# A pad of 32 bytes in place of 96 at the top of SBUF, and another order of scalings and stores in the last tile

## The chip, the cores and the metric

One core of one Trainium2 chip. The metric is device time in microseconds (us) of one execution of the program, the median of several runs.

## What is computed

One encoder layer for 512 positions of width 2048, all in float32:

```python
h = rms_norm(x, norm1_g)
p = h @ w_in                                   # 2048 x 5120
y_a = gelu(u) * (W_s @ rms_norm(gelu(v)) + b_s)        # group A, chunks of 128
y_b = x0 * (K * (v * x1) + d * (v * x1))               # group B, long convolution by FFT
x = x + concat(rms_norm(y_a), rms_norm(y_b)) @ w_out
gv = rms_norm(x, norm2_g) @ ffn_w_up           # 2048 x 11008, gate and value
x = x + (gelu(dwconv3(gate)) * value) @ ffn_w_down     # 5504 x 2048
return rms_norm(x, final_g)
```

## The kernel before, in words

**Exact pairs.** Every big product is made of three TensorE matmuls in a rounded float32 form (`mm3`, L222): each operand is split into a high part and the rest (`hi`/`lo`, `hH`/`hL`, `h2H`/`h2L`, `aH`/`aL`), and high x high, high x rest and rest x high are added up in PSUM. The three lines L224 to L226 are these three. `exact_pair` (L142) makes a split: ScalarE copies the high part (L143), VectorE subtracts (L144).

**Streaming the weights.** `plan` (L88) lists all weight units in the order of use, 2 x 128 rows by up to 512 columns each. `next_unit` (L203) loads a unit some units ahead through SP's queue into one of three `raw` buffers and splits it into one of three `hi` and three `lo` buffers. A unit of 512 columns is 24 matmuls with 128 x 512 results (2 row blocks, 4 column blocks, 3 products).

**Which operand is which.** The first operand of `mm3` is stationary: 128 x 128, 512 bytes per partition, loaded into TensorE ahead of its matmul while the one before still runs. The second is moving: 128 x 512, 2048 bytes per partition.

| stage | lines | stationary | moving |
|---|---|---|---|
| first projections `pa`, 8 calls of `projA` | L540 | `hi`, `lo` | `hH`, `hL` |
| `pv`, 2 calls of `projB` | L579 | `hH`, `hL` | `hi`, `lo` |
| output projection `po` | L842 | `hi`, `lo` | `yh`, `ylo`, then `ybH`, `ybL` |
| feed-forward, gate and value `pa` | L1167 | `hi`, `lo` | `h2H`, `h2L` |
| down projection, Strassen units `sa`, `se`, `sc`, `sg` | L1209 | `aH`, `aL` | `hi`, `lo` |
| down projection, last group `pl` | L1303 | `laH`, `laL` | `lH`, `lL` |

Small matmuls of 256 columns serve the filter and its transform (`fh`, `fw`, `fx`), the convolution (`fw`, `iv`) and the spatial gate (`sg` with `w`, `zH`).

**Where tiles lie.** Pools on the left side of SBUF grow upward, pools on the right side downward from the top, and the first one on the right is a pad, `padr` (L234). In the built program, as bytes within a partition: `hi` lies at 37,824, 41,920 and 46,016 and `lo` at 50,112, 54,208 and 58,304, all 448 above a multiple of 512, and so do `aH` (78,784) and `aL` (93,120). `yh`, `ylo`, `ybH` and `ybL` lie at 192 modulo 512, as do the left-side tables and filter tiles (`tabH`, `invH`, `kH`, `wH`, `zH`). The right side has `hH` (163,712) and `hL` (196,480), later `h2H` and `h2L`, `xacc`, the convolution's spectra (`uH`, `sH`), the gate's `w2`, and at the end `lH`, `lL`, `laH` and `laL`: all at 384 modulo 512.

**Order of the feed-forward.** `ffn_order` (L95) is a list: for each group of four gate and value blocks, 8 gate units (G), 8 value units (V) and the 14 Strassen units (S) of the group before. A group is G G G, then five times S G, then S S, then five times V S, then V V V S S; in the last of eleven groups only three times V S, then five V and four S. The first group has no S.

**The last tile.** For each 128 positions t and each quarter q of the columns, `last_out` (L1288) has VectorE add PSUM to the residual (L1299), ScalarE square it and sum it up (L1300), VectorE multiply it by the gain row `grow` (L1301). When the four quarters of a t are done, `leave` (L1310) makes the factor r (VectorE L1313 and L288, GpSimd's power L289) and scales: quarters 0 and 2 on VectorE (L1320), 1 and 3 on ScalarE (L1318); each engine's stores go out through SP or ScalarE's queue (L1321). Instructions of an engine run in the order that the recording layer gave them; a multiplication must wait for the square that reads the same quarter.

Of the kernel before, what the change touches and what calls it, by code (L numbers as in the profile page):

```python
# [15 lines left out]
ALU = mybir.AluOpType  # L16

P = 128
D = 2048
L = 512  # L20
NT = L // P
# [30 lines left out]
def encoder_kernel(ctx: ExitStack, tc: tile.TileContext, a: dict, out: bass.AP):  # L52
    nc = tc.nc
    ACT, DVE, POOL, PE, SP = nc.scalar, nc.vector, nc.gpsimd, nc.tensor, nc.sync
# [4 lines left out]
    def pool(name, side=None, space=None, stack=None):  # L59
        kw = dict(name=name, bufs=1, reuse_waits="tile")  # L60
        if side:
            kw["side"] = side
        if space:
            kw["space"] = space
        return (stack or ctx).enter_context(tc.tile_pool(**kw))
# [163 lines left out]
    def pad(name, nbytes, side=None, stack=None):  # L229

        pool(name, side=side, stack=stack).tile([P, nbytes // 4], F32, name=name)


    pad("padr", 96, "right")  # L234
    right = ExitStack()
    Apool = pool("A", side="right", stack=right)
    hH = Apool.tile([P, KD, L], F32R, name="hH")
# [48 lines left out]
    def rsqrt(r, ss, n):  # L286

        DVE.tensor_scalar(r, ss, 1.0 / n, EPS, ALU.mult, ALU.add)  # L288
        POOL.tensor_tensor(r, r, nhalf.broadcast_to(list(r.shape)), ALU.pow)  # L289
# [795 lines left out]
    def out_tile(t, q):  # L1085

        return xacc[:, 4 * q : 4 * q + 4, t * P : (t + 1) * P]

    def as_out(ap):
        return ap.rearrange("p (k c) -> p k c", k=4)  # L1090
# [188 lines left out]
    grow, fin = [], {}  # L1279
# [8 lines left out]
    def last_out(t, q):  # L1288

        if q == 0:  # L1290
            if t < 2:
                w = ff.tile([P, D], F32, tag=("aH", "aL")[t], name="fin", bufs=1)
                fin[t] = [w[:, i * 512 : (i + 1) * 512] for i in range(4)]
            else:
                ws = [special["raw"]() for _ in range(2)]
                fin[t] = [ws[i // 2][:, i % 2, :] for i in range(4)]
        o = ps_of.pop(("last", t, q))
        x_ = fin[t][q]
        DVE.tensor_tensor(as_out(x_), out_tile(t, q), as_out(o), ALU.add)  # L1299
        ACT.activation(tmp[q % 2], x_, AF.Square, accum_out=ssf[:, t, q : q + 1])  # L1300
        DVE.tensor_tensor(x_, x_, grow[0][:, q * 512 : (q + 1) * 512], ALU.mult)  # L1301

    def last_mm(t, q, k):  # L1303
        if k == 0:
# [5 lines left out]
    def leave(t):  # L1310

        r = const.tile([P, NT], F32, tag="rc", name="r3", bufs=3)
        DVE.tensor_reduce(r[:, 1:2], ssf[:, t, :], mybir.AxisListType.X, ALU.add)  # L1313
        rsqrt(r[:, 0:1], r[:, 1:2], D)
        for q in range(4):
            x_ = fin[t][q]
            if q % 2:
                ACT.activation(x_, x_, AF.Copy, scale=r[:, 0:1])  # L1318
            else:
                DVE.tensor_scalar(x_, x_, r[:, 0:1], None, ALU.mult)  # L1320
            (ACT if q % 2 else SP).dma_start(out[t * P : (t + 1) * P, q * 512 : (q + 1) * 512], x_)  # L1321

    for q in range(4):
        for k0 in range(0, nf, 2):
            next_unit(("L", k0, q), flush)
            while pieces:
                piece()
            for k in range(k0, min(k0 + 2, nf)):
                for t in range(2):
                    last_mm(t, q, k)  # L1330
        posts.extend(lambda t=t, q=q: last_out(t, q) for t in range(2))
    for t in range(2, NT):
        for q in range(4):
            for k in range(nf):
                last_mm(t, q, k)
            flush()
            last_out(t, q)
            if t == 2 and q % 2:
                leave(q // 2)
            elif t == 3 and q == 1:  # L1340
                leave(2)
    leave(3)
    tail.close()
    fst.close()
# [85 lines left out]
```

## Time and profile before

| | |
|---|---|
| median of 3 runs | 2121.99 us (2121.91 to 2122.37) |
| the profiled execution | 2121.79 us |
| its span, first to last instruction | 2120.0 us |
| TensorE busy | 2097.7 us, 99% |
| VectorE, ScalarE, GpSimd busy | 65%, 36%, 10% |
| mean granted TensorE clock | 0.998 of full |
| HBM read, written | 218.42 MB, 8.39 MB |

The profiled execution lasts 1.8 us longer than its span. TensorE's records overlap: a matmul's record is longer than the distance to the next one's start, so in what follows the pace is read from starts in the timeline and not from lengths.

### The profile page before, as it was taken

How to read it: one execution, taken by the hardware profiler on the slowest of the kernel's cores; microseconds unless marked ns; L12 is line 12 of the kernel's file. 1: busy time of each engine (PE TensorE's matmuls, PEld its weight loads, DVE VectorE, ACT ScalarE, POOL GpSimd, SP SyncE). 2: the span in 40 equal slices, each digit the busy share in tenths (PEclk: the TensorE clock that was granted, in tenths of full speed). 3: DMA queues.
4: the chain of work that ended last, by engine and by line, in shares of the span. 5: the costliest groups of instructions: out<-in, count | busy, mean ns of one | idle time of the engine just before them, and what ended most of it. 6: DMA issues, size and time to landing. Idle time of an engine off the chain costs nothing.

```text
span 2120.0 us, 23470 instructions
## 1 busy us (share of the span) xinstructions
PE 2097.7 (99%) x9374; PEld 1703.6 (80%) x9374; DVE 1376.4 (65%) x1655; ACT 757.2 (36%) x954; POOL 217.9 (10%) x124
## 2 busy tenths in 40 slices
PE   8999999999999999999999999999999999999998
PEld 6888887778888888888888888888888888888886
DVE  6873565556897844765667565675755757666768
ACT  6443542223544432332333232332322323332334
POOL 0330311100004510100101001010100101001000
PEclk9999999999999999999999999999999999999999
DMA  8434332243223432333333333333332333333323
GB/s 293 139 118 132 86 85 89 80 139 113 97 90 129 160 89 80 100 109 95 104 90 99 101 98 103 90 101 98 97 112 87 109 94 101 105 99 91 91 82 134
DMA packets 112697, 228.33 MB, mean 108 GB/s; under 512 B 7147, under 2 KB 14507, under 8 KB 110668
## 3 DMA queue, kind: packets, MB, share of 16 engines
q1 hardware_dynamic: 106096, 214.64, 32.6%
q10 hardware_dynamic: 6492, 12.20, 1.6%
q8 instruction: 73, 1.20, 0.2%
q14 instruction: 36, 0.29, 0.0%
HBM read 218.42 MB, written 8.39 MB: 107 GB/s over the span
## 4 chain that ended last, share of the span: by engine, by line
PE 92%; DVE 5%; ACT 1%; issue 1%; DMA 1%; SPq 0%; ACTq 0%; POOLq 0%; DVEq 0%
PE pa L226 20%; PE pa L224 20%; PE pa L225 20%; PE po L224 2%; PE po L225 2%; PE po L226 2%; PE se L225 2%; PE se L224 2%; PE se L226 2%; PE sa L225 2%; PE sa L224 2%; PE sa L226 2%; PE sc L225 2%; PE sc L224 2%; PE sc L226 2%; PE pv L224 1%
## 5 line engine op out<-in xcount | busy, mean ns | idle before, releaser
L224 PE MATMUL pa<-h2H,hi 128*128 128x512 f32 x1376 | 543.5, 395 | 0.0
L225 PE MATMUL pa<-h2L,hi 128*128 128x512 f32 x1376 | 542.2, 394 | 0.0
L226 PE MATMUL pa<-h2H,lo 128*128 128x512 f32 x1376 | 542.1, 394 | 0.0
L144 DVE TENSOR_TENSOR lo<-raw,hi 128x1024 fp32r<-128x1024 f32 (+2 forms) x289 | 359.6, 1247 | 279.5 <-ACT hi L143 279.1
L143 ACT CAST hi<-raw 128x1024 fp32r<-128x1024 f32 (+2 forms) x289 | 298.6, 1033 | 554.4 <-PE pa L225 266.1
L144 DVE TENSOR_TENSOR lo<-sraw,hi 128x1024 fp32r<-128x1024 f32 x140 | 171.6, 1226 | 336.0 <-ACT hi L143 335.9
L143 ACT CAST hi<-sraw 128x1024 fp32r<-128x1024 f32 x140 | 147.0, 1050 | 490.7 <-PE pa L225 419.1
L226 PEld LDWEIGHTS pa<-h2H,lo 128*128 128x128 f32 x1376 | 257.3, 187 | 63.5
L225 PEld LDWEIGHTS pa<-h2L,hi 128*128 128x128 f32 x1376 | 257.5, 187 | 62.2
L224 PEld LDWEIGHTS pa<-h2H,hi 128*128 128x128 f32 x1376 | 257.5, 187 | 62.2
L1113 POOL TENSOR_TENSOR gg<-gg,r 128x512 f32<-128x512 f32 x43 | 91.1, 2130 | 1193.6 <-ACT gg L1112 1193.6
L224 PE MATMUL pa<-hH,hi 128*128 128x512 f32 x512 | 204.9, 400 | 2.0 <-DVE ev L615 1.2
L226 PE MATMUL pa<-hH,lo 128*128 128x512 f32 x512 | 202.9, 397 | 1.0 <-DVE lo L144 1.0
L225 PE MATMUL pa<-hL,hi 128*128 128x512 f32 x512 | 203.2, 397 | 0.0
L224 PEld LDWEIGHTS pa<-hH,hi 128*128 128x128 f32 x512 | 96.7, 189 | 30.5 <-DVE ev L615 4.2
L226 PEld LDWEIGHTS pa<-hH,lo 128*128 128x128 f32 x512 | 96.6, 189 | 25.5 <-DVE lo L144 2.3
L225 PEld LDWEIGHTS pa<-hL,hi 128*128 128x128 f32 x512 | 96.8, 189 | 21.9
L180 DVE TENSOR_TENSOR sraw<-sraw 128x1024 f32<-128x1024 f32 x80 | 98.8, 1235 | 18.2 <-DMA sraw<-in_ffn_w_down 17.9
L225 PE MATMUL sa<-lo,aH 128*128 128x512 f32 x160 | 62.7, 392 | 0.0
L225 PE MATMUL se<-lo,aH 128*128 128x512 f32 x160 | 62.7, 392 | 0.0
L224 PE MATMUL sc<-hi,aH 128*128 128x512 f32 x160 | 62.4, 390 | 0.1
L225 PE MATMUL sc<-lo,aH 128*128 128x512 f32 x160 | 62.5, 391 | 0.0
(281 smaller groups left out, 3055.1 us busy)
## 6 DMA issues: line engine op xcount, KB each, us to landing
raw<-in_ffn_w_up SPq DMA_DIRECT2D x160, 512.0 KB, 3.7
sraw<-in_ffn_w_down SPq DMA_DIRECT2D x80, 512.0 KB, 3.8
raw<-in_w_in SPq DMA_DIRECT2D x79, 512.0 KB, 3.7
raw<-in_w_out SPq DMA_DIRECT2D x32, 512.0 KB, 3.7
raw<-in_ffn_w_up SPq DMA_DIRECT2D x16, 384.0 KB, 3.3
xn<-in_xN ACTq DMA_DIRECT2D x8, 512.0 KB, 5.0
khat_d<-kh SPq DMA_DIRECT2D x4, 1024.0 KB, 4.3
kh<-khat_d SPq DMA_DIRECT2D x4, 1024.0 KB, 4.8
```

What stands on the lines that cost most here:

```text
L143: ACT.copy(hi, src)
L144: eng.tensor_tensor(lo, src, f32(hi), ALU.subtract)
L180: DVE.tensor_tensor(raws[i], sraws[gi, dp, of], sraws[gi, dp, less], ALU.subtract)
L224: PE.matmul(o, ah, bh, start=start, stop=False, skip_group_check=read)
L225: PE.matmul(o, ah, bl, start=False, stop=False, skip_group_check=read)
L226: PE.matmul(o, al, bh, start=False, stop=stop, skip_group_check=read)
L1113: POOL.tensor_tensor(e, e, r2[0], ALU.mult)
```

## The change

The pad becomes 32 bytes. In the built program every right-side tile then lies 64 bytes higher: `hH` at 163,776, `hL` at 196,544, all `h2`, `lH`, `lL`, `laH`, `laL`, `uH`, `sH` and `w2` at 448 modulo 512. Left-side tiles keep their places. In `leave`, quarters 1 and 2 are scaled on ScalarE, 0 and 3 on VectorE, and all four stores go through SP in the order 0, 1, 3, 2; the last quarter of the last tile isn't multiplied by `grow` ahead of its scaling, but in one fused instruction with it.

```diff
-    pad("padr", 96, "right")
+    pad("padr", 32, "right")
...
-        DVE.tensor_tensor(x_, x_, grow[0][:, q * 512 : (q + 1) * 512], ALU.mult)
+        if (t, q) != (NT - 1, 3):
+            DVE.tensor_tensor(x_, x_, grow[0][:, q * 512 : (q + 1) * 512], ALU.mult)
...
         for q in range(4):
             x_ = fin[t][q]
-            if q % 2:
+            if q == 3 and t == NT - 1:
+                DVE.scalar_tensor_tensor(x_, x_, r[:, 0:1], grow[0][:, 3 * 512 :], ALU.mult, ALU.mult)
+            elif q == 1 or q == 2:
                 ACT.activation(x_, x_, AF.Copy, scale=r[:, 0:1])
             else:
                 DVE.tensor_scalar(x_, x_, r[:, 0:1], None, ALU.mult)
-            (ACT if q % 2 else SP).dma_start(out[t * P : (t + 1) * P, q * 512 : (q + 1) * 512], x_)
+        for q in (0, 1, 3, 2):
+            SP.dma_start(out[t * P : (t + 1) * P, q * 512 : (q + 1) * 512], fin[t][q])
```

On VectorE the change also moves instructions of the last tile. There `sraw_14594` and `sraw_14595` hold quarters 0 and 1, 2 and 3 of t = 2; `sraw_14672` and `sraw_14673` those of t = 3. VectorE before, from the r of t = 2 to the sum for the r of t = 3:

```order
L288 TENSOR_SCALAR r3_14690<-r3_14690 128x1
L1320 TENSOR_SCALAR sraw_14594<-sraw_14594,r3_14690 128x512
L1320 TENSOR_SCALAR sraw_14595<-sraw_14595,r3_14690 128x512
L1299 TENSOR_TENSOR sraw_14672<-xacc_3813,pl_14677 128x512
L1301 TENSOR_TENSOR sraw_14672<-sraw_14672,grow_14408 128x512
L1299 TENSOR_TENSOR sraw_14673<-xacc_3813,pl_14702 128x512
L1301 TENSOR_TENSOR sraw_14672<-sraw_14672,grow_14408 128x512
L1299 TENSOR_TENSOR sraw_14673<-xacc_3813,pl_14715 128x512
L1301 TENSOR_TENSOR sraw_14673<-sraw_14673,grow_14408 128x512 x2
L1313 TENSOR_REDUCE r3_14728<-ssf_14359 128x1
```

VectorE with the change, the same stretch (`pl_14715` is quarter 3, the last that TensorE makes):

```order
L288 TENSOR_SCALAR r3_14690<-r3_14690 128x1
L1302 TENSOR_TENSOR sraw_14672<-sraw_14672,grow_14408 128x512
L1299 TENSOR_TENSOR sraw_14672<-xacc_3813,pl_14677 128x512
L1323 TENSOR_SCALAR sraw_14594<-sraw_14594,r3_14690 128x512
L1323 TENSOR_SCALAR sraw_14595<-sraw_14595,r3_14690 128x512
L1302 TENSOR_TENSOR sraw_14672<-sraw_14672,grow_14408 128x512
L1299 TENSOR_TENSOR sraw_14673<-xacc_3813,pl_14702 128x512
L1302 TENSOR_TENSOR sraw_14673<-sraw_14673,grow_14408 128x512
L1299 TENSOR_TENSOR sraw_14673<-xacc_3813,pl_14715 128x512
L1314 TENSOR_REDUCE r3_14727<-ssf_14359 128x1
```

Before, each multiplication by `grow` stood behind the addition of the quarter that follows; now it stands ahead of it, and the last quarter's is gone. ScalarE over the same stretch, one piece of the difference:

```order
 L1300 ACTIVATE tmp0_5856,ssf_14359<-sraw_14672 128x512
-L1318 ACTIVATE sraw_14594<-sraw_14594,r3_14690 128x512
+L1321 ACTIVATE sraw_14594<-sraw_14594,r3_14690 128x512
+L1321 ACTIVATE sraw_14595<-sraw_14595,r3_14690 128x512
 L1300 ACTIVATE tmp1_5857,ssf_14359<-sraw_14672 128x512
-L1321 DMA out_0<-sraw_14594 128x512
-L1318 ACTIVATE sraw_14595<-sraw_14595,r3_14690 128x512
 L1300 ACTIVATE tmp0_5856,ssf_14359<-sraw_14673 128x512
-L1321 DMA out_0<-sraw_14595 128x512
 L1300 ACTIVATE tmp1_5857,ssf_14359<-sraw_14673 128x512
```

Both scalings of t = 2 now stand ahead of the square of quarter 1 of t = 3, and ScalarE issues no stores.

## Rows read from the trace of the kernel before

**Rows 1.** The page, busy time of each engine, whole span.

```profile
PE 2097.7 (99%) x9374; PEld 1703.6 (80%) x9374; DVE 1376.4 (65%) x1655; ACT 757.2 (36%) x954; POOL 217.9 (10%) x124
```

**Rows 2.** What TensorE waited for: us in total, times, longest us.

```profile
PE hp L358 <- DMA zw<-in_zw: 4.0, 1, 4.0
...
PE pa L224 <- DVE ev L615: 1.2, 4, 0.3
```

**Rows 3.** Groups of TensorE instructions: count, busy us, mean ns of one.

```profile
L224 PE MATMUL pa<-h2H,hi 128*128 128x512 f32 x1376 | 543.5, 395 | 0.0
```

**Rows 4.** TensorE's timeline, two Strassen units and three gate units: start, us.

```profile
1198.37 0.39 PE L224 MATMUL sg<-hi,aH 128*128 128x512 f32 x1
...
1201.11 0.39 PE L224 MATMUL sc<-hi,aH 128*128 128x512 f32 x1
...
1203.83 0.39 PE L224 MATMUL pa<-h2H,hi 128*128 128x512 f32 x1
...
1220.63 0.39 PE L224 MATMUL sa<-hi,aH 128*128 128x512 f32 x1
```

**Rows 5.** The same view, output projection.

```profile
691.82 0.39 PE L224 MATMUL po<-ybH,hi 128*128 128x512 f32 x1
...
701.34 0.39 PE L224 MATMUL po<-ybH,hi 128*128 128x512 f32 x1
```

**Rows 6.** The same view, last group of the down projection.

```profile
2095.07 0.39 PE L224 MATMUL pl<-lH,laH 128*128 128x512 f32 x1
...
2099.83 0.39 PE L224 MATMUL pl<-lH,laH 128*128 128x512 f32 x1
```

**Rows 7.** The same view, first projections with the weights stationary.

```profile
380.13 0.39 PE L224 MATMUL pa<-hH,hi 128*128 128x512 f32 x1
...
389.93 0.39 PE L224 MATMUL pa<-hH,hi 128*128 128x512 f32 x1
```

**Rows 8.** The same view, `pv`, and 18 filter transforms of 256 columns.

```profile
144.78 0.39 PE L224 MATMUL pv<-hi,hH 128*128 128x512 f32 x1
...
146.61 0.39 PE L226 MATMUL pv<-hi,hL 128*128 128x512 f32 x1
146.84 0.28 PE L224 MATMUL fw<-kH,tabH 128*128 128x256 f32 x1
...
148.88 0.28 PE L226 MATMUL fx<-kH,tabL 128*128 128x256 f32 x1
```

**Rows 9.** The same view, 18 transforms of the convolution's input, 256 columns.

```profile
515.28 0.28 PE L224 MATMUL fw<-uH,tabH 128*128 128x256 f32 x1
...
517.28 0.28 PE L226 MATMUL fw<-uH,tabL 128*128 128x256 f32 x1
```

**Rows 10.** Groups of TensorE instructions in the first 63 us, first of three alike.

```profile
L224 PE MATMUL pa<-hH,hi 128*128 128x512 f32 x64 | 26.8, 419 | 0.8 <-ACT hi L143 0.8
```

**Rows 11.** Busy us (and count) by engine, then granted clock, DMA share, GB/s.

```profile
1200.00:1400.00 200.00, 200.00 (x865) 161.66 (x864) 131.19 (x152) 66.16 (x75) 11.31 (x6) 1.00 0.32 98
```

**Rows 12.** Timeline of the end, ScalarE, VectorE and GpSimd.

```profile
2107.38 0.72 ACT L1318 ACTIVATE sraw<-sraw,r 128x512 f32<-128x512 f32 x1
...
2110.91 0.69 DVE L1299 TENSOR_TENSOR sraw<-xacc,pl 128x512 f32<-128x512 f32 x1 [0.25 <-PE pl L226]
...
2111.63 0.63 ACT L1300 ACTIVATE tmp<-sraw 128x512 f32<-128x512 f32 x1 [0.79 <-DVE sraw L1299]
...
2112.39 0.69 DVE L1301 TENSOR_TENSOR sraw<-sraw,grow 128x512 f32<-128x512 f32 x1 [0.19 <-ACT tmp L1300]
2113.00 0.15 DVE L1313 TENSOR_REDUCE r<-ssf 128x1 f32<-128x4 f32 x1
...
2113.50 0.55 POOL L289 TENSOR_TENSOR r<-r,nhalf 128x1 f32<-128x1 f32 x1 [6.16 <-DVE r L288]
2114.08 0.88 DVE L1320 TENSOR_SCALAR sraw<-sraw,r 128x512 f32<-128x512 f32 x2 [0.75 <-POOL r L289]
2114.08 1.33 ACT L1318 ACTIVATE sraw<-sraw,r 128x512 f32<-128x512 f32 x2 [1.73 <-POOL r L289]
```

## The prediction

> **What bounds the kernel now.** The page's busy table comes first: TensorE is busy 99% of the span [rows 1], so time is won only if its matmuls come closer together or if something outside them gets shorter. Next, the list of what TensorE waits for: eleven lines, from 4.0 us down to 0.2, together 13.0 us [rows 2]. None names a tile of the feed-forward part, and the largest belong to the start and to the convolution. So the question is how far apart matmuls start when nothing makes them wait. The busy column can't tell, because records overlap (0.39 us long, started every 0.23); the timeline's starts can.
>
> All big matmuls are 128 x 512, with a fresh 128 x 128 stationary block loaded for each. Their pace has two levels:
> - gate and value units of the feed-forward: 72 starts from 1203.83 to 1220.63, 233.3 ns each [rows 4]. Stationary operand `hi`/`lo` (448 modulo 512), moving operand `h2` (384): they differ by 64 bytes.
> - the first projections: 42 starts from 380.13 to 389.93, 233.3 ns [rows 7], again 448 against 384.
> - the output projection: 42 starts from 691.82 to 701.34, 226.7 ns [rows 5]. The loop is the same (four banks, three matmuls per bank, weights stationary); the moving operand lies at 192, a difference of 256.
> - the last group of the down projection: 21 starts from 2095.07 to 2099.83, 226.7 ns [rows 6]. Both operands lie at 384, difference 0.
> - Strassen units, both at 448, difference 0: 12 starts from 1201.11 to 1203.83, 226.7 ns; but the unit ahead, which directly follows a gate unit, takes 2.74 us for 12, not 2.72 [rows 4].
>
> [...] What goes with the slow level is the offset of 64 bytes between the moving operand and the weights being loaded. [...]
>
> **The change part by part.** The pad moves every tile of the right side up by 64 bytes: `hH`, `hL` and all `h2` go from 384 to 448, onto the offset of `hi` and `lo`. Left tiles stay.
>
> 1. Gate and value units. 3 x 1376 = 4128 matmuls [rows 3], from difference 64 to 0. I take the pace of the rows with difference 0, 226.7 ns [rows 4, 6]: 4128 x 6.67 ns = **-27.5 us**. Bounds: no gain (233.3) and 226.7, the fastest steady pace that any row shows. The low end, because two kinds of matmul with difference 0 show it, over all four residues of the stationary block modulo 2048.
> 2. Strassen units that directly follow a gate or value unit. The order list gives 12 such units in each of nine groups and 10 in the last, 118. Their extra 0.02 us [rows 4] looks like a settling from one offset to the other; with equal offsets throughout it should go: **-2.4 us**, bounds 0 and -2.4. The reverse bound: if the settling belongs to the change of unit, it now appears at gate units too, up to 11 x 16 x 0.02 = +3.5 us. I take none.
> 3. First projections with weights stationary: 8 x 16 x 4 x 3 = 1536 matmuls, 191 of them in the first 63 us (three forms, 64, 64 and 63 [rows 10]). The other 1345: 1345 x 6.67 = **-9.0 us**. The few waits there for an evacuated bank [rows 2] are counted from TensorE's own last matmul, so they move along with it. For the 191 early ones the gain lies between 0 and 1.3 us, since transfers and splits pace that stretch (their mean length is 419 ns, that of the gate units 395 [rows 3, 10]); I take **-0.6 us**.
> 4. The two `pv` groups, roles swapped, difference 64 the other way: 8 starts from 144.78 to 146.61, 228.8 ns [rows 8]. At difference 0: 384 x 2.1 = **-0.8 us**; bounds 0 and -0.8.
> 5. The 256-wide matmuls that touch a right-side tile: 96 forward, 192 inverse, 64 spatial-gate, 352 in all, come to a difference of 256. The only rows near are 117.6 ns at difference 320 [rows 9] and 120.0 at difference 0 [rows 8]; 2.4 ns either way is 0.8 us either way. I take 0, since at 512 columns a difference of 256 is as fast as any.
> 6. The last tile. Here the order on the engines decides. The change takes one multiplication by `grow` from ahead of the last sum of squares: 0.61 us from its start to the reduction's [rows 12]. Taken alone this would be -0.6 us. But in the new order VectorE multiplies quarter 2 *before* it adds quarter 3, and both r-scalings of tile 2 on ScalarE now stand ahead of the square of quarter 1. Worked through in order, with durations of rows 12: ScalarE starts tile 2's scalings at 2107.38 as before (their r is unchanged) and, at 1.33 for two, is free at 2108.71; from a square's start to the multiplication that waits for it go 0.76, so VectorE multiplies quarter 1 from 2109.47 to 2110.15 and adds quarter 2 until 2110.75; another 0.76 later it multiplies quarter 2, from 2111.53 to 2112.2, and only then adds quarter 3, until 2112.8; before, that addition began at 2110.91, right behind TensorE. Square (0.76), reduction and power (1.08 from the reduction to the scalings) follow, and the scalings begin at 2114.66, not 2114.08: +0.58 us. What follows (scaling and four stores, 5.9 us to the end of the span) I keep. All four stores now go through SP; the fused scale of quarter 3 and the later issue of the last store could add 0.5 us more. **+0.6 us**, bounds -0.6 and +1.1.
>
> SP gains eight issues, ScalarE loses eight; behind them stand only stores, and TensorE waits for neither.
>
> What hides the rest: with TensorE 2% faster VectorE must deliver as much in less time. In 200 us of the middle it is busy 131, ScalarE 66, DMA 0.32 [rows 11]; in 196 us that still fits.
>
> Sum: -27.5 - 2.4 - 9.0 - 0.6 - 0.8 + 0.6 = -39.7 us. Against the profiled execution's 2121.8 us this is 2082.1; the median of the runs lies 0.2 above that execution, so 2082.3 us.
>
> **The rivals.** Changes within 0.2% (4.2 us) can't be told from none.
> - *Forecast, offset 0 is as fast as in the Strassen units:* chance 0.85. Its own range from the bounds above: all of the early gain, the 256-wide gain and a short tail give 2079.5; no settling gain, 3.5 us of new settling, no early or `pv` gain, slower 256-wide ones and the long tail give 2091.0.
> - *In between:* regular units settle at the `pv` pace of 228.8 ns [rows 8], because the switching between kinds keeps disturbing them. Then (4128 + 1345) x 4.6 ns = 25 us less, about 2097. For it: `pv` shows that such a level exists. Against: Strassen units reach 226.7 within one unit. 0.06.
> - *Placement does nothing:* the two levels come from something else that goes with `h` (the distance between the tiles, how they were written). Then only the tail counts: 2121.8 + 0.6 = 2122.4, which is no change. [...] For it: no row has `h` at another offset. Against: `pv` reads the same `h` and is faster; `lH` and `laH` lie in the same region at 384 and run at 226.7 [rows 6]. 0.06.
> - *Slower:* equal offsets make both reads hit the same place every cycle. The 256-wide rows hint at it: 120.0 ns where both lie at 192 [rows 8], 117.6 at another difference [rows 9]. Were 512-wide matmuls with `h` moving to pay 2.4 ns over today's pace, 6048 x 2.4 = 14.5 us more, about 2137. It decides from about 234.0 ns, where 6048 x 0.7 passes 4.2 us. Against: difference 0 at 512 columns runs at 226.7 twice [rows 4, 6]. 0.03.
>
> **How the numbers follow.** The likeliest case gives 2082.3 us. Its own range, 2079.5 to 2091.0, holds its 0.85 almost whole and so about 8 in 10; the others are left out. Faster by over 0.2%: 0.85 + 0.06 = 0.91; within 0.2%: 0.06; slower: 0.03.
>
> **What would show it.** Right: in gate units 72 starts take 16.3 us and not 16.8; a Strassen unit behind them takes 2.72; the first projections' 42 starts take 9.52; the last tile's addition of quarter 3 starts over a microsecond behind TensorE's end. Wrong: starts still 233 ns apart, or new waits of TensorE for `hi` or `lo` in the feed-forward, or the last scalings 3.2 us or less behind TensorE's last end, as before (2110.91 to 2114.08 [rows 12]; the forecast is 3.75).

## The result

The changed kernel takes 2087.4 us (median of 4 runs, 2086.55 to 2088.0) where the kernel before, run beside it, took 2121.97: a ratio of 0.9836, 95% interval 0.9819 to 0.9853. The forecast was 2082.3 with a range of 2079.5 to 2091.0. The profiled execution took 2086.55 us with a span of 2084.7, which is 35.3 us less than the 2120.0 of before.

### The profile page after: what moved, and what is told of

It is laid out like the page before. It is cut to its first block, busy times and chain, and to the rows that moved or that the text cites. A ratio compares the mean times of both kernels' runs of the same rounds, so it can differ in the third digit from the quotient of the medians.

```text
span 2084.7 us, 23478 instructions
## 1 busy us (share of the span) xinstructions
PE 2059.8 (99%) x9374; PEld 1706.9 (82%) x9374; DVE 1374.5 (66%) x1654; ACT 758.6 (36%) x954; POOL 215.4 (10%) x124
## 4 chain that ended last, share of the span: by engine, by line
PE 90%; DVE 7%; ACT 1%; issue 1%; DMA 1%; POOL 0%; ACTq 0%; SPq 0%; POOLq 0%; DVEq 0%
PE pa L226 19%; PE pa L224 19%; PE pa L225 19%; PE po L224 2%; PE po L226 2%; PE po L225 2%; PE se L225 2%; PE se L226 2%; PE se L224 2%; PE sa L225 2%; PE sa L226 2%; PE sa L224 2%; PE sc L225 2%; PE sc L224 2%; PE sc L226 2%; PE pv L224 1%
## 5 line engine op out<-in xcount | busy, mean ns | idle before, releaser
L224 PE MATMUL pa<-h2H,hi 128*128 128x512 f32 x1376 | 536.7, 390 | 0.0
L226 PE MATMUL pa<-h2H,lo 128*128 128x512 f32 x1376 | 535.6, 389 | 0.0
L225 PE MATMUL pa<-h2L,hi 128*128 128x512 f32 x1376 | 535.4, 389 | 0.0
L226 PE MATMUL sc<-hi,aL 128*128 128x512 f32 x160 | 62.3, 389 | 0.0
L224 PE MATMUL sa<-hi,aH 128*128 128x512 f32 x160 | 62.2, 389 | 0.0
```

The costliest lines, as they stand in the source:

```text
L224: PE.matmul(o, ah, bh, start=start, stop=False, skip_group_check=read)
L225: PE.matmul(o, ah, bl, start=False, stop=False, skip_group_check=read)
L226: PE.matmul(o, al, bh, start=False, stop=stop, skip_group_check=read)
```

## The profile after

The page's busy table [rows 1] again: same instructions, one VectorE instruction less, TensorE still busy 99%, in a shorter span.

```profile
PE 2059.8 (99%) x9374; PEld 1706.9 (82%) x9374; DVE 1374.5 (66%) x1654; ACT 758.6 (36%) x954; POOL 215.4 (10%) x124
```

TensorE's timeline of the changed kernel, the same instructions as in [rows 4, 7, 9] (start in us, then the length of the record):

```profile
375.60 0.39 PE L224 MATMUL pa<-hH,hi 128*128 128x512 f32 x1
385.12 0.39 PE L224 MATMUL pa<-hH,hi 128*128 128x512 f32 x1
...
507.88 0.28 PE L224 MATMUL fw<-uH,tabH 128*128 128x256 f32 x1
509.92 0.28 PE L226 MATMUL fw<-uH,tabL 128*128 128x256 f32 x1
...
1180.92 0.39 PE L224 MATMUL sg<-hi,aH 128*128 128x512 f32 x1
1183.64 0.39 PE L224 MATMUL sc<-hi,aH 128*128 128x512 f32 x1
...
1186.36 0.39 PE L224 MATMUL pa<-h2H,hi 128*128 128x512 f32 x1
1202.68 0.39 PE L224 MATMUL sa<-hi,aH 128*128 128x512 f32 x1
```

The 72 starts of the gate units now take 16.32 us where they took 16.80, so 226.7 ns each and not 233.3. The Strassen unit directly behind gate units takes 2.72 us, not 2.74. The 42 starts of the first projections take 9.52 us, not 9.80. The 18 transforms of 256 columns went the other way: 2.04 us, not 2.00.

What TensorE waits for in the changed kernel (us in total, times, longest us), the lines that answer to [rows 2]:

```profile
PE hp L358 <- DMA zw<-in_zw: 4.1, 1, 4.1
PE fw L225 <- DVE kL L144: 1.9, 2, 1.7
PE iv L224 <- ACT sH L143: 1.8, 3, 1.0
PE pa L226 <- DVE lo L144: 1.5, 3, 0.6
PE pa L224 <- DVE ev L615: 1.5, 4, 0.4
...
PE hp L358 <- ACT h L372: 0.8, 1, 0.8
```

Before, these six were 4.0, 1.6, 2.2, 1.0, 1.2 and 0.2 us. Four of them that hang on VectorE or ScalarE, all amid the first projections (`fw`, both `pa`, and `hp` for `h`), grew, by 1.7 us together.

The last tile, VectorE, ScalarE and GpSimd [rows 12], and TensorE's last matmul:

```profile
2070.34 0.69 DVE L1302 TENSOR_TENSOR sraw<-sraw,grow 128x512 f32<-128x512 f32 x1
2070.52 0.91 POOL L289 TENSOR_TENSOR r<-r,nhalf 128x1 f32<-128x1 f32 x1 [3.75 <-PE pl L226]
...
2071.47 1.34 ACT L1321 ACTIVATE sraw<-sraw,r 128x512 f32<-128x512 f32 x2 [1.16 <-POOL r L289]
...
2074.20 0.39 PE L226 MATMUL pl<-lH,laL 128*128 128x512 f32 x1
2075.59 0.69 DVE L1302 TENSOR_TENSOR sraw<-sraw,grow 128x512 f32<-128x512 f32 x1 [0.85 <-ACT tmp L1300]
2076.20 0.68 DVE L1299 TENSOR_TENSOR sraw<-xacc,pl 128x512 f32<-128x512 f32 x1
...
2077.72 0.16 DVE L1314 TENSOR_REDUCE r<-ssf 128x1 f32<-128x4 f32 x1 [0.85 <-ACT tmp L1300]
2078.82 0.49 DVE L1323 TENSOR_SCALAR sraw<-sraw,r 128x512 f32<-128x512 f32 x1 [0.75 <-POOL r L289]
```

TensorE's last matmul in the kernel before:

```profile
2110.48 0.39 PE L226 MATMUL pl<-lH,laL 128*128 128x512 f32 x1
```

The addition of quarter 3 begins 2.00 us behind TensorE's last start (0.43 before), because VectorE stands in front of the multiplication of quarter 2 until its square is done. The scalings begin 4.62 us behind that start (3.60 before), and the span ends 10.5 us behind it (9.5 before).

**Where the 35.3 us come from.** TensorE's 9374 matmuls stand in the same order in both traces, so they can be matched one by one, and the difference of every start to the next start added up by stage. A step over 250 ns (over 160 for 256 columns) is put down as a wait. The last tile is the way from TensorE's last start to the span's end. The figures are rounded; they add up to the span's -35.3 but for that.

| part | forecast, us | measured, us |
|---|---|---|
| gate and value units, pace | -27.5 | -26.8 |
| Strassen units behind them | -2.4 | -2.3 |
| first projections, pace (late, early) | -9.0, -0.6 | -8.1, -0.8 |
| `pv` | -0.8 | -0.8 |
| waits of the first projections | 0 | +1.8 |
| 256-wide matmuls, pace | 0 | +0.9 |
| waits in convolution and output projection | 0 | -0.5 |
| last tile | +0.6 | +1.0 |
| rest | 0 | +0.2 |

## Experiments

The theory: TensorE's pace follows from the difference, modulo 512 bytes, of the addresses of the moving operand and of the weights, and the tail's order is worth a microsecond the wrong way. Rivals: the absolute place of `h` counts, or some other neighbour of the tiles that the pad moves; the price falls off with the difference; the tail's order gains.

**1. The pad alone.**

```diff
-    pad("padr", 96, "right")
+    pad("padr", 32, "right")
```

> The pad of 32 bytes alone, last tile as before. Offset theory (all the gain is the pad's, and the new order of the last tile costs what its trace shows: 10.54 us from TensorE's last start to the end of the span against 9.50): 1.0 us less than the changed kernel, 2085.5 to 2087.0, with 9.5 us behind TensorE's last start. Rival (the last tile's order gains, and the pad does a little less): 2088 or more.

Measured: 2085.4 us (2084.82 to 2087.06, 5 runs), ratio 0.9828, interval 0.9815 to 0.9842. TensorE's last matmul starts at 2074.13, as in the changed kernel (2074.20), and the span ends 9.5 us behind it, as before the change. So the whole gain is the pad's.

**2. The tail alone**, the changed kernel with the old pad.

```diff
-    pad("padr", 32, "right")
+    pad("padr", 96, "right")
```

> The last tile's new order alone, pad of 96 bytes. Offset theory with an order that costs: 2123.0 us, 1.0 more than before, gate units at 233.3 ns a start. Rival (the order gains 0.6): 2121.4. Rival (the order changes nothing that the end waits for): 2122.0.

Measured: 2123.17 us (2122.82 to 2124.42, 11 runs), ratio 1.0006, interval 0.9997 to 1.0015: that interval can't tell this from nothing, though each of the 11 runs is longer than each of the 15 of the kernel before beside them (up to 2122.58). The trace shows where the time is: the span ends 10.49 us behind TensorE's last start, 1.0 more than before, and GpSimd's power for tile 2 takes 0.91 us again:

```profile
2108.47 0.91 POOL L289 TENSOR_TENSOR r<-r,nhalf 128x1 f32<-128x1 f32 x1 [3.75 <-PE pl L226]
```

**3. The weights moved instead of `h`.** The pad stays at 96 bytes, and a tile of 448 bytes ahead of the pool of the streamed weights brings `hi` and `lo` to 384, where `h` lies in the kernel before. Every left-side tile behind it moves by as much, so `aH` and `aL` still lie as `hi` and `lo` do.

```diff
+    pool("padw").tile([P, 448 // 4], F32, name="padw")
     wp = pool("wp")
```

> Before, with a pad of 448 bytes ahead of the weight buffers: h stays at 384 modulo 512, hi and lo move from 448 to 384, so their difference is 0 at another absolute place. If the difference sets the pace: gate units at 226.7 ns, about 2086 us. If the place of h sets it (384 slow, 448 fast): 233.3 ns and about 2122 us.

Measured: 2085.32 us (2084.98 to 2087.35, 4 runs), ratio 0.9829, interval 0.9815 to 0.9842. The 72 starts of the gate units, in TensorE's timeline of this kernel (its lines stand one further down):

```profile
1188.18 0.39 PE L225 MATMUL pa<-h2H,hi 128*128 128x512 f32 x1
1204.50 0.39 PE L225 MATMUL sa<-hi,aH 128*128 128x512 f32 x1
```

16.32 us, 226.7 ns each. `h` did not move, and the gain is the same as with the pad alone. The absolute place of `h` falls; the difference between the two operands stays.

**4 to 7. Other differences.** The kernel before with pads of 64, 160, 288 and 480 bytes, each an edit of that one line, which puts `h` at 416, 320, 192 and 0 modulo 512, the weights staying at 448.

```diff
-    pad("padr", 96, "right")
+    pad("padr", 64, "right")
```

> Before with a pad of 64 bytes: h at 416, a difference of 32 bytes. [...] If any difference short of a larger step is the same clash: 233.3 ns and 2122 us. If only 64 is bad: 226.7 ns and 2086 us.

> The kernel before with a pad of 160 bytes: h lies 128 bytes away from the streamed weights (modulo 512), where it lay 64 away before. [...]

> Pad of 288 bytes: h lies 256 bytes from the weights. [...] A pace of 233.3 ns (2122 us) would mean that the output projections are fast for another reason than their difference, and that only equal addresses help.

> Pad of 480 bytes: h lies 64 bytes on the other side of the weights. If the sign does not matter, 233.3 ns and 2122 us. If it does, the value and gate projection of the kernel before, which had its operands 64 bytes apart the other way and started every 228.8 ns, shows the price: about 2 ns for each of the 5500 matmuls that read h, so 2097 us (2093 to 2100). If only the one side clashes at all, 2085.4 us.

The same 72 gate starts in TensorE's timelines, pad 64:

```profile
1205.44 0.40 PE L224 MATMUL pa<-h2H,hi 128*128 128x512 f32 x1
1222.25 0.39 PE L224 MATMUL sa<-hi,aH 128*128 128x512 f32 x1
```

Pad 160:

```profile
1203.63 0.40 PE L224 MATMUL pa<-h2H,hi 128*128 128x512 f32 x1
1220.42 0.39 PE L224 MATMUL sa<-hi,aH 128*128 128x512 f32 x1
```

Pad 288:

```profile
1185.98 0.39 PE L224 MATMUL pa<-h2H,hi 128*128 128x512 f32 x1
1202.30 0.39 PE L224 MATMUL sa<-hi,aH 128*128 128x512 f32 x1
```

Pad 480, with the Strassen unit directly behind gate units, and the one after that:

```profile
1189.86 0.40 PE L224 MATMUL sg<-hi,aH 128*128 128x512 f32 x1
1192.63 0.39 PE L224 MATMUL sc<-hi,aH 128*128 128x512 f32 x1
1195.35 0.40 PE L224 MATMUL pa<-h2H,hi 128*128 128x512 f32 x1
1211.85 0.40 PE L224 MATMUL sa<-hi,aH 128*128 128x512 f32 x1
```

| moving `h` against the weights, bytes | pad | start to start, ns | time, us |
|---|---|---|---|
| 32 below | 64 | 233.4 | 2124.06 |
| 64 below | 96 (before) | 233.3 | 2121.97 |
| 128 below | 160 | 233.2 | 2120.5 |
| 256 apart | 288 | 226.7 | 2085.39 |
| the same | 32 (after) | 226.7 | 2085.4 with the old tail |
| 64 above | 480 | 229.1 | 2106.42 |

The runs of the four other pads are single ones; their paces rest on thousands of matmuls each. In the gate units the price does not fall off between 32 and 128 bytes, and it is gone at 256. The expectation for 64 bytes on the other side missed by 9 us. Its pace was nearly as expected from `pv`, whose moving weights lay 64 above `h` [rows 8]: 229.1 ns for 228.8. What was left out is that the Strassen unit directly behind gate units now takes 2.77 us (1189.86 to 1192.63) where it takes 2.72 with equal addresses, 118 x 0.05 = 5.9 us; the unit after it takes 2.72 again. And `pv`, now 64 the other way, starts every 233 ns, another 384 x 6 ns = 2.3 us.

`pv` also shows what the table can't, moving operands 32 and 128 bytes above. With the pads of 64 and 160 bytes its moving weights lie that far above `h`. From the first line of each pair to the second it is nine starts, pad 64:

```profile
144.83 0.39 PE L224 MATMUL pv<-hi,hH 128*128 128x512 f32 x1
146.93 0.28 PE L224 MATMUL fw<-kH,tabH 128*128 128x256 f32 x1
```

Pad 160:

```profile
144.74 0.39 PE L224 MATMUL pv<-hi,hH 128*128 128x512 f32 x1
146.83 0.28 PE L224 MATMUL fw<-kH,tabH 128*128 128x256 f32 x1
```

That is 233.3 and 232.2 ns a start. So lying above is not cheaper in itself: of the three differences above, 64 alone is.

**8. The pad, and only the fused scale of the last quarter.** Before's order of additions and multiplications and its two store queues stay.

```diff
+        if (t, q) != (NT - 1, 3):
+            DVE.tensor_tensor(x_, x_, grow[0][:, q * 512 : (q + 1) * 512], ALU.mult)
...
+        end = t == NT - 1
+        for q in (0, 1, 3, 2) if end else range(4):
             x_ = fin[t][q]
+            on_act = q in (1, 2) if end else q % 2
+            if end and q == 3:
+                DVE.scalar_tensor_tensor(x_, x_, r[:, 0:1], grow[0][:, 3 * 512 :], ALU.mult, ALU.mult)
...
+            (ACT if on_act else SP).dma_start(out[t * P : (t + 1) * P, q * 512 : (q + 1) * 512], x_)
```

> Pad of 32 bytes, and of the tail's change only the fused scale of the last quarter; before's order of additions and multiplications on VectorE and before's two queues of stores stay. In the kernel with the pad alone the last sum of squares is there 0.6 us before VectorE's reduction begins, since the last multiplication stands between. If that multiplication is what the last tile can save, the scalings begin 3.0 us behind TensorE's last start and not 3.6, the span's end lies 8.9 us behind it (9.5 with the pad alone, 10.5 in the changed kernel), and the time is 2084.8 us (2084.2 to 2085.4). If fusing itself costs (a longer last operation of 0.75 us for 0.49 us), the end stays at 9.5 us and the time at 2085.4 us.

Measured: 2084.64 us (2084.33 to 2085.17, 5 runs), ratio 0.9823, interval 0.9809 to 0.9836: the lowest median of all, below both kernels of this case. VectorE, GpSimd and ScalarE at the end, in this kernel (TensorE's last start is at 2074.19):

```profile
2074.61 0.69 DVE L1299 TENSOR_TENSOR sraw<-xacc,pl 128x512 f32<-128x512 f32 x1 [0.26 <-PE pl L226]
2075.22 0.68 DVE L1302 TENSOR_TENSOR sraw<-sraw,grow 128x512 f32<-128x512 f32 x1
...
2076.09 0.16 DVE L1314 TENSOR_REDUCE r<-ssf 128x1 f32<-128x4 f32 x1 [0.19 <-ACT tmp L1300]
...
2077.18 1.33 ACT L1323 ACTIVATE sraw<-sraw,r 128x512 f32<-128x512 f32 x2 [1.12 <-POOL r L289]
2077.58 0.74 DVE L1321 SCALAR_TENSOR_TENSOR sraw<-sraw,r,grow 128x512 f32<-128x512 f32 x1
```

The addition of quarter 3 begins 0.42 us behind TensorE's last start again, the scalings 2.99 us behind it, and the span ends at 8.7 us (9.5 with the pad alone, 10.5 in the changed kernel). The span's end is 0.2 us nearer than the 8.9 us that was expected. Of the 2.8 us to the changed kernel's median the traces show 1.9, all of it in the last tile; where the rest comes from they do not show. The intervals of the ratios overlap, though the five runs here all lie below the four of the changed kernel.

**9. The 256-wide operands put back.** Two pads of 64 bytes more, on top of the kernel of experiment 8, bring the convolution's and the spatial gate's right-side operands to 384 again.

```diff
+    pad("padm", 64, "right", ms)
     mp = pool("mix", side="right", stack=ms)
...
+    pad("padd", 64, "right", ds_)
     dp = pool("long", side="right", stack=ds_)
```

> The kernel with the fused last quarter, and two pads of 64 bytes more, ahead of the pool of the spatial gate's operands and ahead of the pool of the convolution's, so that these operands (w2, uH, uL, sH, sL) lie at 384 again, as before the change, and the h tiles stay at 448. If the 352 matmuls of 256 columns pay for their difference of 256, they return to 117.6 ns from 120 and TensorE's time falls by 0.9 us: 2083.7 us, and 18 starts of the forward transform take 2.00 us and not 2.04. If their pace came from something else, 2084.6 us and 2.04 us. If the waits for VectorE's splits in the convolution take the gain back, the pace returns and the time does not: 2.00 us and 2084.6 us.

Measured: 2084.67 us (2084.28 to 2086.47, 5 runs), ratio 0.9822, interval 0.9809 to 0.9836: no change against experiment 8. The 18 transforms, in TensorE's timeline:

```profile
509.61 0.28 PE L224 MATMUL fw<-uH,tabH 128*128 128x256 f32 x1
...
511.61 0.28 PE L226 MATMUL fw<-uH,tabL 128*128 128x256 f32 x1
```

2.00 us, as before the change, so their pace does hang on the difference. But in the list of waits the inverse transform waits for ScalarE's `sH` as before again:

```profile
PE iv L224 <- ACT sH L143: 2.2, 3, 1.1
```

From the output projection's first start to the feed-forward's first, the matched 256-wide steps take 0.5 us less than in experiment 8 and the waits 0.4 more. The third outcome of the expectation held in that stage: TensorE's extra time had been filling a wait. The 64 matmuls of the spatial gate came back only in part, with `w2` at 384 again: 117.4 ns on average, for 118.8 in experiment 8 and 114.5 in the kernel before. What else they paid for stays open. The profiled execution of this kernel took 2086.47, the longest of its five; the wait for `hi` in its first 63 us is 2.4 us long, and 0.8 in experiment 8, whose profiled execution took 2084.64.

## Why the prediction was right, and which terms missed

In the profiled execution's own terms the forecast was 4.5 us short (2082.1 against 2086.55), inside its range; the table above says where. That the range held the result was in part luck. Its slow end, 2091.0, holds 2.4 us for a settling that stays behind gate units and 3.5 for one that moves to them, and neither came; without these it would have ended at 2085.0, below the measured 2087.4. For the waits of the first projections, the largest of what did come, it had no room. (Added up from its own terms the range is 2079.6 to 2090.9, 0.1 us off at either end. And one of the eleven waits of [rows 2], `pl` for `lL` with 0.4 us, does belong to the feed-forward part; no term hangs on that.)

1. **Gate and value units: right.** 226.7 ns, as the rows with difference 0 had it; 26.8 of 27.5 us. The rival "in between" at 228.8 ns falls. So does "placement does nothing": experiments 1 and 3 move one operand each and gain 36.8 and 36.9 us. The gate units start every 233.3 ns in the kernel before and every 226.7 in the changed one, with the same instructions in the same order and a granted clock of 1.00 in both (from 1200 to 1400 us before, from 1180 to 1380 in the changed kernel). Why a difference of 64 bytes costs the 6.7 ns, no run shows.
2. **Settling of Strassen units: right** in size and in cause. It is 0.02 us a unit behind gate units with `h2` 64 below, 0.05 with `h2` 64 above, and none where all operands lie alike. The reverse bound of +3.5 us fell: the gate units start every 226.8 ns on average over all 4113 steps without a wait.
3. **First projections: the mechanism right, the size too large.** The pace gave 8.1 and 0.8 us. The 8.1 are short of 9.0 chiefly because not every start came down to 226.7 ns: 126 of the 1323 steps without a wait still take over 228 ns, 0.7 us in all above 226.7, and 71 of them are among the first twelve behind matmuls of 256 columns. That is a settling that the term left out. The waits are the larger miss. The step that failed there is the sentence that the waits there "are counted from TensorE's own last matmul, so they move along with it". One stretch between two waits shows it. VectorE and TensorE in the kernel before:

```profile
322.06 9.05 DVE L628 SCALAR_TENSOR_TENSOR v<-ev,cols,v 128x127 f32<-128x127 f32 x15
322.27 0.50 PE L224 MATMUL pa<-hH,hi 128*128 128x512 f32 x1 [0.29 <-DVE ev L615]
331.04 3.43 DVE L144 TENSOR_TENSOR lo<-raw,hi 128x1024 fp32r<-128x1024 f32 x2
332.31 0.50 PE L226 MATMUL pa<-hH,lo 128*128 128x512 f32 x1 [0.20 <-DVE lo L144]
```

and in the changed kernel:

```profile
318.74 9.06 DVE L628 SCALAR_TENSOR_TENSOR v<-ev,cols,v 128x127 f32<-128x127 f32 x15
318.95 0.50 PE L224 MATMUL pa<-hH,hi 128*128 128x512 f32 x1 [0.36 <-DVE ev L615]
327.72 3.44 DVE L144 TENSOR_TENSOR lo<-raw,hi 128x1024 fp32r<-128x1024 f32 x2
328.99 0.50 PE L226 MATMUL pa<-hH,lo 128*128 128x512 f32 x1 [0.45 <-DVE lo L144]
```

Restart to restart is 10.04 us in both. Between them VectorE goes through its filter steps, 9.05 us without a pause, and then makes the `lo` that TensorE needs; the faster matmuls end earlier and wait longer. Such a stretch gave nothing back. In the first 63 us the waits took back 0.6 us, and 1.2 in the rest of the first projections, 0.4 of it at the filter's transform, where `fw` waits for `kL`.

4. **`pv`: right**, 0.8 us.
5. **256-wide matmuls: the wrong value of the two bounds.** I took 0 "since at 512 columns a difference of 256 is as fast as any"; they pay 0.9 us of pace (120 ns for 117.6), the upper bound of 0.8 and a little. Experiment 9 shows, for the transforms, that this is the difference's price, and that about half of the 0.9 filled a wait; for the 64 matmuls of the spatial gate it shows that in part only.
6. **Last tile: the sign right, the size short**, +1.0 for +0.6, near the end of its bounds. The order was worked through rightly: the addition of quarter 3 is what got late. The step that failed is "ScalarE starts tile 2's scalings at 2107.38 as before (their r is unchanged)". That start was 3.10 us ahead of TensorE's last one and is now 2.73 ahead, 0.37 later, because the power on GpSimd takes 0.91 us where it took 0.54; in the new order VectorE multiplies by `grow` beside it (2070.34 to 2071.03). GpSimd in the kernel before:

```profile
2106.81 0.54 POOL L289 TENSOR_TENSOR r<-r,nhalf 128x1 f32<-128x1 f32 x1 [3.74 <-PE pl L226]
```

Everything behind it in the chain of squares and additions is late by that. What follows the scalings was kept at 5.9 us, and so it was (5.92). But with the same scalings and before's two queues, experiments 8 and 9 end 5.7 us behind them (5.68 and 5.67), so four stores through SP cost about 0.2 us, by one profile of each kernel.

## What to carry to other kernels

Where matmuls run back to back, read start to start in the timeline (226.7 ns in the changed kernel's gate units) and not the lengths of records (0.39 us), and sort the paces by the addresses of the two operands modulo 512 bytes; two levels in one trace, here 233.3 ns at 64 bytes below and 226.7 at 0 and 256, are a price list for free. Sum such a gain over stretches between waits, not over matmuls: where another engine works without a pause from one wait to the next, as VectorE did here for 9.05 us of the 10.04 from restart to restart, TensorE's gain turns into a longer wait. In an in-order tail, an instruction taken out is worth what it held up only if the rest keeps its order: in experiment 8, with before's order, the span's end came from 9.5 to 8.7 us behind TensorE's last start; with the new order it went to 10.5.

## What the runs showed of the hardware that was not expected

- A difference of 32 bytes costs a 512-wide matmul as much as one of 64 or 128 (233.2 to 233.4 ns), and 256 nothing (226.7). 64 above costs less than 64 below, 229.1 ns for 233.3, but 32 and 128 above cost 233.3 and 232.2. Since 0 and 256 are alike at this width, these runs do not tell a period of 512 bytes from one of 256.
- At 256 columns it is otherwise: differences of 0 and 256 give 120 ns, one of 320 gives 117.6. Why the two widths differ stays open.
- GpSimd's 128 x 1 power for tile 2 took 0.91 us in the two kernels where VectorE began a multiplication by `grow` 0.18 us ahead of it (the changed kernel and experiment 2), and 0.54 with before's order (the kernel before, experiments 1, 4 and 8). In the changed kernel it would have ended at 2071.06 with 0.54; it ended at 2071.43, 0.40 behind the end of the multiplication. At tile 0 of the changed kernel the power began 0.10 us ahead of the multiplication; there the power took 0.55 us and the multiplication its usual 0.69. Neither case was tried by itself, and no run shows why the power was longer in the one.

```profile
2063.83 0.55 POOL L289 TENSOR_TENSOR r<-r,nhalf 128x1 f32<-128x1 f32 x1 [62.25 <-DVE r L1314]
2063.93 0.69 DVE L1302 TENSOR_TENSOR sraw<-sraw,grow 128x512 f32<-128x512 f32 x1
```
